# Two of five chunk pairs of a SwiGLU layer as seven block products, with the second matrix product's steps among them and TensorE's order pinned

## The chip, the cores and the metric

The kernel runs on one core of a Trainium2 chip. The metric is the device time of one execution in microseconds. Its engines are named as in the profile: PE (TensorE: matmuls and transposes), PEld (its weight loads, which overlap matmuls), DVE (VectorE), ACT (ScalarE), POOL (GpSimd) and SP (SyncE, whose queue starts nearly all DMAs here). L12 is line 12 of the kernel.

## The reference

Two layers of a decoder trunk, each a feed-forward network (FFN), a token mixer and another FFN, with a normalization after each. 256 tokens, width 1024, FFN width 2816; all in float32.

```python
def swiglu(x, wg, wu, wd):
    return (jax.nn.silu(x @ wg) * (x @ wu)) @ wd
...
for l in range(DEPTH):
    x = layer_norm(ALPHA * x + 0.5 * swiglu(x, ffn_wg[l, 0], ffn_wu[l, 0], ffn_wd[l, 0]), ln_g[l, 0], ln_b[l, 0])
    m = token_mix(x, w_in[l], w_out[l], ...)
    x = layer_norm(ALPHA * x + m, ln_g[l, 1], ln_b[l, 1])
    x = layer_norm(ALPHA * x + 0.5 * swiglu(x, ffn_wg[l, 1], ffn_wu[l, 1], ffn_wd[l, 1]), ln_g[l, 2], ln_b[l, 2])
```

The change concerns the four FFNs alone.

## The kernel before

**Tiles.** The 256 tokens are two token tiles t = 0, 1 of 128. The FFN width is cut into 11 chunks of 256. For a chunk, "gate and up" is one product: x (128 tokens, 1024 wide) times a 1024x512 block that holds 256 columns of wg and 256 of wu. It takes eight contraction steps of 128 and gives one PSUM bank of 128x512. Its first half goes through silu, the product of both halves is the chunk's hidden value hh (128x256). hh is transposed, and "down" multiplies it by 256 rows of wd into two banks (acc) that gather the result of all eleven chunks.

**Precision.** Each float32 matmul is three matmuls in a shorter format (fp32r): a number is split into a high part and a low part, and high x high, high x low and low x high are added (`mm3`, L183-186). So each weight tile must be split. `split_half` (L157-168) does it: SP's queue loads a raw tile of 128x1024 (512 KB, L163) into one of three buffers `raw`, ACT writes the high part `wh` (L166), DVE subtracts it for the low part `wl` (L167). There are eight buffers of `wh` and eight of `wl`. The raw buffer is free again when DVE has read it, the split buffers when PE has used them for both token tiles. x is transposed by PE and split in the same way (`make_xT`, L217, with the split at L189 and L190); so is hh (L212, then L189/L190).

**Units.** A list of units, of two weight tiles each, fixes the order of the weights: for chunk c its two gate-and-up units (q = 0, 1: the two halves of the contraction), then the down unit of chunk c-1. `unit(t)` (L177) hands out the next one to token tile t and makes one more ahead (`AHEAD = 1`).

**Order.** `ffn_steps` (L263-325) is a generator for one token tile: gate and up of a chunk (`glu`), the down of the chunk before, the transposes of hh (`h_T`). `ffn` (L762-803) runs the two generators alternately, up to three steps apart. The two token tiles use the same weight unit soon after each other. The program is written in this order, but a scheduler then places each engine's instructions by its own estimate of times, so that transposes stand in the midst of other products. Banks of PSUM: two acc for each token tile, and one g and one tr for each, where tr takes transposes.

**Ends.** After the last down `layer_norm` (L238-260) adds and normalizes x in two halves on DVE, with small steps elsewhere, and `make_xT` transposes it for the next layer. In the second FFN of layer 0 the next user is the first FFN of layer 1 (around 490 us in the trace). In the first FFN some constants of the mixer (`late_constants`) are loaded from SP's queue in its middle.

The three lines that all matmuls of the products come from:

```python
PE.matmul(ps, xh, wh, start=start, stop=False)
PE.matmul(ps, xh, wl, start=False, stop=False)
last_pe[0] = PE.matmul(ps, xl, wh, start=False, stop=stop)
```

## Time and profile before

| | |
|---|---|
| median of 3 runs | 1008.43 us (1007.34 to 1010.68) |
| profiled execution | 1007.14 us |
| its span | 1005.4 us |
| TensorE's granted clock | 0.998 |
| DMA moved | 178.80 MB, 178 GB/s on average |

The page gives the busy time of each engine, and in 40 slices of the span how busy each was and what the DMAs moved. The four FFNs lie at about 20 to 186, 322 to 489, 500 to 688 and 816 to 996 us; the mixers lie between the first and second and between the third and fourth, and the second FFN is followed directly by the third. A group row reads: line, engine, operation, out <- in, shape, count, then busy time and the mean of one in ns, then how long the engine was idle just before and what ended that. A row of the timeline reads: start and duration in us, engine, line, operation, and in brackets the wait before it and what ended it. A matmul of 512 columns is shown with 0.39 us, but these overlap: the pace is the distance of their starts.

### The profile page before, as it was taken

To read this page: it belongs to the slowest core of one execution; us is meant where nothing else is said; L and a number is where in the kernel's file an instruction comes from. 1 tells how busy PE (TensorE), PEld (TensorE's weight loads), DVE (VectorE), ACT (ScalarE), POOL (GpSimd) and SP (SyncE) were. 2 spreads that over 40 slices of the span, in tenths; PEclk is the share of its full clock that TensorE was granted. 3 is DMA by queue.
4 is the path that set the end of the run, shared out by engine and by line. 5 is a ranking of instruction groups with operands and counts; after the bars stand their busy time and mean duration, and the time that the engine had idled before them with its cause. 6 is when DMAs were issued, how large, how long until landed. Compare 5 with 4: busy or idle time off the path is not lost.

```text
span 1005.4 us, 12883 instructions
## 1 busy us (share of the span) xinstructions
PE 991.1 (99%) x4755; PEld 804.1 (80%) x4755; DVE 630.8 (63%) x1051; ACT 491.1 (49%) x788; POOL 35.4 (4%) x50
## 2 busy tenths in 40 slices
PE   8999999999999999999999999999999999999996
PEld 5888888878778888888878888887778788888885
DVE  5545645688869555555775545459888685545455
ACT  5535544366744444444444444435666454444440
POOL 0000000020001000000000000001100010000000
PEclk9999999999999999999999999999999999999999
DMA  7787665365515655556475565645524176565541
GB/s 234 236 254 255 214 195 170 120 196 173 161 55 172 228 186 190 187 188 189 146 243 197 174 197 178 196 151 189 180 84 147 45 230 207 181 195 179 194 152 42
DMA packets 51871, 178.80 MB, mean 178 GB/s; under 512 B 6624, under 2 KB 7648, under 8 KB 51552
## 3 DMA queue, kind: packets, MB, share of 16 engines
q1 hardware_dynamic: 49968, 171.23, 53.2%
q0 software_dynamic: 1840, 6.75, 2.3%
q8 instruction: 37, 0.61, 0.2%
q14 instruction: 26, 0.21, 0.1%
HBM read 176.91 MB, written 1.05 MB: 177 GB/s over the span
## 4 chain that ended last, share of the span: by engine, by line
PE 89%; DVE 5%; DMA 3%; issue 1%; ACT 1%; SPq 0%; DVEq 0%; ACTq 0%
PE g L184 15%; PE g L186 15%; PE g L185 15%; PE acc L184 11%; PE acc L186 11%; PE acc L185 11%; PE tr L212 4%; DMA raw<-in_wgu 2%; PE acc L203 2%; DVE wl L167 2%; PE tr L203 1%; ACT wh L166 1%; PE tr L458 1%; PE acc L200 1%; DMA x<-in_x 1%
## 5 line engine op out<-in xcount | busy, mean ns | idle before, releaser
L167 DVE TENSOR_TENSOR wl<-raw,wh 128x1024 fp32r<-128x1024 f32 (+2 forms) x321 | 388.4, 1212 | 255.6 <-ACT wh L166 244.2
L166 ACT ACTIVATE wh<-raw 128x1024 fp32r<-128x1024 f32 (+2 forms) x321 | 336.1, 1049 | 286.6 <-PE acc L186 103.3
L184 PE MATMUL g<-wh,xh 128*128 128x512 f32 (+1 forms) x736 | 292.6, 398 | 0.0
L186 PE MATMUL g<-wh,xl 128*128 128x512 f32 (+1 forms) x736 | 286.1, 389 | 0.0
L185 PE MATMUL g<-wl,xh 128*128 128x512 f32 (+1 forms) x736 | 285.4, 388 | 0.4 <-DVE wl L167 0.4
L186 PEld LDWEIGHTS g<-wh,xl 128*128 128x128 f32 x736 | 138.4, 188 | 28.2
L185 PEld LDWEIGHTS g<-wl,xh 128*128 128x128 f32 x736 | 138.7, 189 | 26.9 <-DVE wl L167 1.5
L184 PEld LDWEIGHTS g<-wh,xh 128*128 128x128 f32 x736 | 138.4, 188 | 25.9 <-ACT wh L166 0.7
L184 PE MATMUL acc<-wh,hi 128*128 128x512 f32 x352 | 138.5, 393 | 0.0
L186 PE MATMUL acc<-wh,lo 128*128 128x512 f32 x352 | 137.7, 392 | 0.0
L185 PE MATMUL acc<-wl,hi 128*128 128x512 f32 x352 | 137.3, 390 | 0.0
L186 PEld LDWEIGHTS acc<-wh,lo 128*128 128x128 f32 x352 | 66.1, 188 | 13.6
L184 PEld LDWEIGHTS acc<-wh,hi 128*128 128x128 f32 x352 | 66.1, 188 | 13.5 <-ACT hi L189 0.4
L185 PEld LDWEIGHTS acc<-wl,hi 128*128 128x128 f32 x352 | 66.2, 188 | 13.4
L282 ACT ACTIVATE sg<-g 128x256 f32<-128x256 f32 x80 | 30.5, 382 | 75.2 <-PE g L186 74.9
L189 ACT ACTIVATE hi<-tr 128x256 fp32r<-128x256 f32 x88 | 32.9, 374 | 66.4 <-PE tr L212 66.4
L190 DVE TENSOR_TENSOR lo<-tr,hi 128x256 fp32r<-128x256 f32 x88 | 37.0, 421 | 39.2 <-ACT hi L189 39.2
L185 PE MATMUL acc<-wl,xh 128*128 128x512 f32 x128 | 51.2, 400 | 0.5 <-DVE wl L167 0.5
L184 PE MATMUL acc<-wh,xh 128*128 128x512 f32 x128 | 51.2, 401 | 0.0
L186 PE MATMUL acc<-wh,xl 128*128 128x512 f32 x128 | 51.0, 398 | 0.0
L284 DVE SCALAR_TENSOR_TENSOR hh<-sg,g 128x256 f32<-128x256 f32 x80 | 33.4, 417 | 26.5 <-ACT sg L282 26.5
L252 POOL TENSOR_TENSOR ve<-ve,mhalf 128x1 f32<-128x1 f32 x12 | 11.5, 957 | 755.9 <-DVE ve L251 755.9
(207 smaller groups left out, 826.8 us busy)
## 6 DMA issues: line engine op xcount, KB each, us to landing
raw<-in_wgu SPq DMA_DIRECT2D x175, 512.0 KB, 3.9
raw<-in_wd SPq DMA_DIRECT2D x88, 512.0 KB, 3.9
raw<-in_win SPq DMA_DIRECT2D x32, 512.0 KB, 4.0
raw<-in_wout SPq DMA_DIRECT2D x16, 512.0 KB, 3.6
lnp_ln_g<-in_ln_g POOLq DMA_DIRECT2D x5, 512.0 KB, 5.1
lnp_ln_b<-in_ln_b POOLq DMA_DIRECT2D x5, 512.0 KB, 5.7
raw<-in_win SPq DMA_DIRECT2D x8, 296.0 KB, 2.9
x<-in_x SPq DMA_DIRECT2D x4, 256.0 KB, 4.9
```

The source lines that it names most:

```text
L166: ACT.activation(out=wh[:, s], in_=raw[:, s], func=AF.Copy)
L167: DVE.tensor_sub(out=wl[:, s], in0=raw[:, s], in1=wh[:, s].bitcast(F32))
L184: PE.matmul(ps, xh, wh, start=start, stop=False)
L185: PE.matmul(ps, xh, wl, start=False, stop=False)
L186: last_pe[0] = PE.matmul(ps, xl, wh, start=False, stop=stop)
L189: ACT.activation(out=hi, in_=src, func=AF.Copy)
L190: DVE.tensor_sub(out=lo, in0=src, in1=hi.bitcast(F32))
L203: PE.matmul(out, lhsT, rhs, start=False, stop=True, skip_group_check=True)
L212: last_pe[0] = PE.transpose(p[:, i * 128:(i + 1) * 128], s, ident)
L252: POOL.tensor_tensor(out=ve[:, 1:2], in0=ve[:, 0:1], in1=mhalf[:, 0:1], op=ALU.pow)
L282: ACT.activation(out=sg, in_=ps[:, 0:256], func=AF.Silu)
L284: DVE.scalar_tensor_tensor(out=hh, in0=sg, scalar=0.5, in1=ps[:, 256:512], op0=ALU.mult, op1=ALU.mult)
```

## The change

**Grouping.** The eleven chunks are now groups: pairs (0,1), (2,3), (6,7) and the single chunk 10 are computed as before ("n"); the pairs (4,5) and (8,9) are done in seven block products ("s").

**Block products.** For a pair of chunks, x is a 2x2 matrix of blocks: token tile t by half q of the contraction, 128x512 each. The weights are a 2x2 matrix too: half q by chunk, 512x512 each. That is eight block products of 4 steps x 3 matmuls = 12 matmuls. The Strassen-Winograd scheme needs seven: three of plain blocks of x with a plain or combined block of weights, and four of sums of blocks of x. Sums of x are made once per FFN (`make_sums`, and copies of the transposed x at L307 and L310 in `make_xT`). Differences of weights are made for each pair, in float32, ahead of the split (`less`, L143). To that end four raw tiles are kept for longer, in buffers that the mixer had to itself: two `fa` and, from the tag pT, two `fc`. The sums of results are made from banks by DVE with high priority (L452, 453, 459, 464, 469), with two copies on ACT.

**Downs.** In the groups "n" no down is done. The four downs due stand between the block products of the next "s" group, in the order of `SEVEN`: product, down, product, down, two products, down, two products, down, product. Downs of chunks 8, 9 and 10 come at the end, for token tile 0 and then for tile 1 (`end`). hh of a pair is transposed by four transposes into one bank (`h_T`), where it was two and two.

**Order pinned, banks.** From the pair (2,3) to chunk 10 (`middle`) each matmul of these products is pinned (`tc.keep_in_program_order`): the scheduler leaves PE's order as written. Units are then made three ahead, otherwise one. The four banks g0, g1, tr0, tr1 are now a free list in an FFN. The constants of the mixer are loaded after the group (6,7) of the first FFN.

The diff, cut to its core:

```diff
+GROUPS = (("n", 0, 1), ("n", 2, 3), ("s", 4, 5), ("n", 6, 7), ("s", 8, 9), ("n", 10))
+SEVEN = (None, 0, None, 1, None, None, 2, None, None, 3, None)
-    "P": (("P",), 3),
+    "P": (("P",), 4),
+    def seven(l, f, c):
...
+        def less(a, b, to):
+            for x, y, z in zip(a, b, to):
+                DVE.tensor_sub(out=z, in0=x, in1=y)
...
+        def f1():
+            for h, a in enumerate(gate_up(l, f, c, 0)):
+                load(A, [a], mix, name="fa", tag=f"qs{h}", bufs=1)
+            return parts(A)
+        def f2():
+            load(B, gate_up(l, f, c + 1, 0), wp, name="raw", bufs=3)
+            less(B, A, A)
+            return parts(A)
+        def f3():
+            load(C, gate_up(l, f, c + 1, 1), mix, name="fc", tag="pT", bufs=3)
+            less(C, B, B)
+            return parts(B)
+        def f4():
+            less(C, A, A)
+            return parts(A)
+        def f5():
+            load(E, gate_up(l, f, c, 1), wp, name="raw", bufs=3)
+            return parts(E)
+        def f6():
+            return parts(C)
+        def f7():
+            less(E, A, A)
+            return parts(A)
...
+    def make_sums(sums):
+        out = []
+        s1, a11, a12, a21 = sums["s"], sums[0, 0], sums[0, 1], sums[1, 0]
...
+        parts(s1, 0)
+        DVE.tensor_sub(out=s1, in0=s1, in1=a11)
+        DVE.tensor_sub(out=a21, in0=a11, in1=a21)
+        parts(a21, 1)
+        parts(s1, 2)
+        DVE.tensor_sub(out=a12, in0=a12, in1=s1)
+        parts(a12, 3)
...
+            self.free = [("g", 0), ("g", 1), ("tr", 0), ("tr", 1)]
...
+            (w1, b1), (w5, b5) = self.bank(), self.bank()
+            self.product(b1, a[0][0])
+            with tc.high_priority():
+                c11 = f32("c11")
+                ACT.activation(out=c11, in_=b1, func=AF.Copy)
+            for t in range(2):
+                self.h_T(t, c // 2 - 1)
+            down()
+            self.product(b5, s1)
+            down()
+            w7, b7 = self.bank()
+            self.product(b7, s3)
+            self.product(b1, s2, False)
+            with tc.high_priority():
+                u = f32("u")
+                ACT.activation(out=u, in_=b1, func=AF.Copy)
+                c22 = f32("c22")
+                DVE.tensor_add(out=c22, in0=b5, in1=u)
+                DVE.tensor_add(out=c22, in0=b7, in1=c22)
+            self.gated(1, c + 1, c22)
+            down()
+            w2, b2 = self.bank()
+            self.product(b2, a[0][1])
+            with tc.high_priority():
+                DVE.tensor_add(out=c11, in0=b2, in1=c11)
+            self.gated(0, c, c11)
+            self.product(b5, s4, False)
...
+            down()
+            self.product(b7, a[1][1], False)
...
+        def end(self, t, sums):
+            self.down(t, NCH - 3)
+            self.h_T(t, NCH // 2)
+            self.down(t, NCH - 2)
+            self.down(t, NCH - 1)
+            layer_norm(t, self.accs[t], self.l, self.i)
+            if (self.l, self.i) != (L - 1, 2):
+                make_xT(t, sums=sums)
```

**PE in the middle of an FFN.** Before, a down of one chunk (acc from wh, wl and hi, lo) is followed by the two transposes of one chunk's hh and another down:

```order
L184 MATMUL acc_337<-wh,hi 128x512
L185 MATMUL acc_337<-wl,hi 128x512
L186 MATMUL acc_337<-wh,lo 128x512
L184 MATMUL acc_338<-wh,hi 128x512
L185 MATMUL acc_338<-wl,hi 128x512
L186 MATMUL acc_338<-wh,lo 128x512
L212 MATMUL tr_629<-ident,hh 128x128 x2
L184 MATMUL acc_370<-wh,hi 128x512
L185 MATMUL acc_370<-wl,hi 128x512
```

Now, at the start of the first block stage, the first block product (L418, into bank tr_545) ends, the transposes of two chunks stand together for each token tile, and the first down follows:

```order
L418 MATMUL tr_545<-wh,xh_100 128x512
L418 MATMUL tr_545<-wl,xh_100 128x512
L418 MATMUL tr_545<-wh,xl_101 128x512
L487 MATMUL g_573<-ident,hh_443 128x128 x4
L487 MATMUL g_582<-ident,hh_459 128x128 x4
L264 MATMUL acc_591<-wh,hi 128x512
L265 MATMUL acc_591<-wl,hi 128x512
L266 MATMUL acc_591<-wh,lo 128x512
```

What moved: a block product, which needs no hh, now stands ahead of the transposes, and these come in fours. L264-266 are the lines that were L184-186.

**PE at the end of the second FFN.** Before, token tile 0's new x (x_102) is transposed among the last downs of tile 1, which come after a whole chunk's product into g_4377:

```order
L184 MATMUL acc_3183<-wh,hi 128x512
L185 MATMUL acc_3183<-wl,hi 128x512
L186 MATMUL acc_3183<-wh,lo 128x512
L184 MATMUL acc_3184<-wh,hi 128x512
L212 MATMUL tr_4363<-ident,x_102 128x128 x4
L212 MATMUL acc_4370<-ident,x_102 128x128 x4
L212 MATMUL tr_4406<-ident,hh 128x128 x2
L185 MATMUL acc_3184<-wl,hi 128x512
```

Now tile 1 has only its three downs (8, 9, 10) left, and the transposes (x_98 is tile 0's x) stand in the second of them:

```order
L487 MATMUL tr_4434<-ident,hh_4325 128x128 x2
L264 MATMUL acc_3423<-wh,hi 128x512
L265 MATMUL acc_3423<-wl,hi 128x512
L266 MATMUL acc_3423<-wh,lo 128x512
L264 MATMUL acc_3424<-wh,hi 128x512
L265 MATMUL acc_3424<-wl,hi 128x512
L292 MATMUL tr_4404<-ident,x_98 128x128 x4
L292 MATMUL acc_4413<-ident,x_98 128x128 x4
L266 MATMUL acc_3424<-wh,lo 128x512
```

The whole chunk's product of 24 matmuls no longer stands in between.

**DVE at the first block stage.** Before, low parts of weights (L167) alternate with low parts of the transposed hh (L190) and gates (L284):

```order
L190 TENSOR_TENSOR lo<-tr_363,hi 128x256
L167 TENSOR_TENSOR wl<-raw,wh 128x1024
L190 TENSOR_TENSOR lo<-tr_384,hi 128x256
L167 TENSOR_TENSOR wl<-raw,wh 128x1024 x4
L284 SCALAR_TENSOR_TENSOR hh<-sg,g_391 128x256
```

Now the differences (L143) stand there too, and low parts come from the kept tiles (L220) as well as from fresh ones (L232):

```order
L143 TENSOR_TENSOR raw<-fc,raw 128x1024
L143 TENSOR_TENSOR fa<-fc,fa 128x1024
L270 TENSOR_TENSOR lo<-g_573,hi 128x512
L270 TENSOR_TENSOR lo<-g_582,hi 128x512
L143 TENSOR_TENSOR fa<-fc,fa 128x1024
L232 TENSOR_TENSOR wl<-raw,wh 128x1024
L220 TENSOR_TENSOR wl<-raw,wh 128x1024 x2
L220 TENSOR_TENSOR wl<-fa,wh 128x1024 x2
L232 TENSOR_TENSOR wl<-raw,wh 128x1024 x2
```

Each kept tile is written over by its difference, so `fa` and `raw` appear as outputs of L143.

**SP's queue at the start.** Before, raw tiles are loaded in the order of their use:

```order
L163 DMA raw<-in_wgu 128x1024 x7
L163 DMA raw<-in_wd 128x1024 x2
L163 DMA raw<-in_wgu 128x1024 x4
L163 DMA raw<-in_wd 128x1024 x2
L163 DMA raw<-in_wgu 128x1024 x4
```

Now the tiles that the first block stage keeps stand among the first groups' loads:

```order
L228 DMA raw<-in_wgu 128x1024 x3
L139 DMA fa<-in_wgu 128x1024 x2
L228 DMA raw<-in_wgu 128x1024 x3
L139 DMA fc<-in_wgu 128x1024 x2
L228 DMA raw<-in_wgu 128x1024 x3
L139 DMA fc<-in_wgu 128x1024
L228 DMA raw<-in_wgu 128x1024 x6
L228 DMA raw<-in_wd 128x1024 x2
```

The third `fc` is the second block stage's first tile, in the third buffer of its tag. Over the whole program PE has 96 matmuls of 512 columns fewer, 3687 where there were 3783.

More of the change, by code (lines that the diff above doesn't have):

```diff
@@ L172, in split_weights @@
         while len(made) < min(n, len(units)):
-            made.append([split_half(src, w) for src, w in units[len(made)]])
+            made.append(units[len(made)]())
     pos = [0, 0]
+    ahead = [1]
     def unit(t):
@@ L179, in unit, with both, pe @@
         pos[t] += 1
-        split_weights(u + 1 + AHEAD)
+        split_weights(u + 1 + ahead[0])
         return made[u]
+    def both():
+        u = unit(0)
+        assert unit(1) is u
+        return u
+    pinned = [False]
+    def pe(ins):
+        if pinned[0]:
+            tc.keep_in_program_order(ins)
+        last_pe[0] = ins
     def mm3(ps, xh, xl, wh, wl, start, stop):
-        PE.matmul(ps, xh, wh, start=start, stop=False)
-        PE.matmul(ps, xh, wl, start=False, stop=False)
-        last_pe[0] = PE.matmul(ps, xl, wh, start=False, stop=stop)
+        pe(PE.matmul(ps, xh, wh, start=start, stop=False))
+        pe(PE.matmul(ps, xh, wl, start=False, stop=False))
+        pe(PE.matmul(ps, xl, wh, start=False, stop=stop))
     def split(hi, lo, src):
@@ L223, in make_xT, with parts @@
             split(xh[:, 4 * q:4 * q + 4, :], xl[:, 4 * q:4 * q + 4, :], p.rearrange("p (a b) -> p a b", a=4))
+            if sums is not None:
+                if (t, q) != (1, 1):
+                    f = sums[t, q] = mix.tile([128, 512], F32, name=f"a{t}{q}", tag=("c40", "c41", "at011")[2 * t + q], bufs=1)
+                    ACT.activation(out=f, in_=p, func=AF.Copy)
+                else:
+                    f = sums["s"] = mix.tile([128, 512], F32, name="s1", tag="vblk", bufs=1)
+                    DVE.tensor_add(out=f, in0=p, in1=sums[1, 0])
+    def make_sums(sums):
+        out = []
+        s1, a11, a12, a21 = sums["s"], sums[0, 0], sums[0, 1], sums[1, 0]
+        big = cst.tile([128, 2, 2, 4, 128], F32R, name="sb", tag="s_w1")
+        def parts(f, i):
+            tl = cst.tile([128, 2, 4, 128], F32R, name=f"sa{i}", tag=("ksh", "ksl")[i]) if i < 2 else big[:, i - 2]
+            split(tl[:, 0], tl[:, 1], f.rearrange("p (a b) -> p a b", a=4))
+            out.append((tl[:, 0], tl[:, 1]))
+        parts(s1, 0)
[5 more added lines that the diff above has]
+        parts(a12, 3)
+        s1, s3, s2, s4 = out
+        return s1, s2, s3, s4
     lnp = {}
@@ L761, in run, with ffn @@
             k += 1
-    def ffn(l, i):
-        gens = [ffn_steps(t, l, i) for t in range(2)]
-        n = 3 * NCH
-        done = [0, 0]
-        def go(t, k):
-            run(gens[t], k)
-            done[t] += k
+    def ffn(l, i, sums, after):
+        f = Ffn(l, i, sums)
         if (l, i) == (0, 0):
@@ L773, in ffn @@
             load_x(0, 0)
-            make_xT(0, (0,))
+            make_xT(0, (0,), sums)
             with tc.issue_after(last_pe[0].ins):
                 warm_up()
-            first = split_half(*units[0][0], 2, (lambda: load_x(0, 1), lambda: load_x(1, 0)))
+            first = split_half(gate_up(0, 0, 0, 0)[0], 1024, 2, (lambda: load_x(0, 1), lambda: load_x(1, 0)))
             with tc.issue_after(last_pe[0].ins):
-                make_xT(0, (1,))
+                make_xT(0, (1,), sums)
             load_x(1, 1)
-            made.append([first, split_half(*units[0][1])])
-            gens[0] = ffn_steps(0, l, i)
-            go(0, 1)
+            made.append([first, split_half(gate_up(0, 0, 0, 0)[1], 1024)])
+            f.glu(0, 0, 0)
             with tc.issue_after(x1_after[0].ins):
-                make_xT(1)
-            gens[1] = ffn_steps(1, l, i)
-            go(1, 1)
-            go(0, 1)
-            go(1, 1)
-            go(0, 1)
-        else:
-            go(0, LEAD)
-        while done[0] < n - LEAD + 1:
-            go(1, min(2, done[0] - done[1] - 1) if done[0] - done[1] > 2 else 1)
-            if done[0] - done[1] <= 1:
-                go(0, 1)
-            if not m0 and done[0] >= 12:
-                with tc.issue_after(last_dma[0].ins):
-                    late_constants()
-                    m0.append(Mix(0))
-                    ln_params(0, 0)
-        go(0, n - done[0])
-        return gens[1], n - done[1]
+                make_xT(1, sums=sums)
+            f.glu(1, 0, 0)
+            f.glu(0, 0, 1)
+            f.glu(1, 0, 1)
+            f.glu(0, 1, 0)
+        else:
+            f.glu(0, 0, 0)
+            f.glu(0, 0, 1)
+            f.glu(0, 1, 0)
+            f.glu(1, 0, 0)
+            f.glu(1, 0, 1)
+        f.glu(0, 1, 1)
+        f.glu(1, 1, 0)
+        f.glu(1, 1, 1)
+        f.middle()
+        for t in range(2):
+            f.end(t, after)
     m0 = []
-    rest = None
+    sums = {}
     for l in range(L):
-        rest = ffn(l, 0)
-        run(*rest)
+        ffn(l, 0, sums, None)
         m = m0[0] if l == 0 else Mix(l)
@@ L828, in build @@
             assert next(g, "end") == "end"
-        rest = ffn(l, 2)
-        run(*rest)
+        nxt = {}
+        ffn(l, 2, m.sums, nxt)
+        sums = nxt
 def _layout(inp):
```

225 lines of the change are left out of this document (156 added, 69 removed).

## The prediction

> **What bounds the kernel now.** I read the page's busy times first, then TensorE's list of waits, then a dense stretch of the timeline.
>
> ```profile
> PE 991.1 (99%) x4755; PEld 804.1 (80%) x4755; DVE 630.8 (63%) x1051; ACT 491.1 (49%) x788; POOL 35.4 (4%) x50
> L186 PEld LDWEIGHTS g<-wh,xl 128*128 128x128 f32 x736 | 138.4, 188 | 28.2
> L212 PE MATMUL tr<-ident,hh 128*128 128x128 f32 x176 | 33.8, 274 | 1.3 <-DVE hh L284 1.3
> ```
>
> ```profile
> PE tr L212 <- DVE hh L284: 1.3, 3, 0.6
> PE acc L102 <- DVE zw L105: 1.2, 1, 1.2
> PE acc L212 <- DMA x<-in_x: 1.1, 1, 1.1
> ...
> PE tr L212 <- DVE x L257: 0.2, 1, 0.2
> ```
>
> A busy share of 99% may hide gaps, since overlapping matmuls are counted to modelled ends. So the waits matter more: the longest total on one cause is 1.3 us in 1005.4. The pace settles it: starts of matmuls with 512 columns in the middle of the third feed-forward layer (FFN):
>
> ```profile
> 600.73 0.39 PE L185 MATMUL acc<-wl,hi 128*128 128x512 f32 x1
> ...
> 602.09 0.39 PE L185 MATMUL acc<-wl,hi 128*128 128x512 f32 x1
> ```
>
> Six matmuls in 1.36 us are 0.2267 us each, back to back. The other engines of the same FFN wait for TensorE: this is ACT, about to split the next weight tile.
>
> ```profile
> 602.07 1.06 ACT L166 ACTIVATE wh<-raw 128x1024 fp32r<-128x1024 f32 x1 [2.74 <-PE acc L186]
> 603.43 1.06 ACT L166 ACTIVATE wh<-raw 128x1024 fp32r<-128x1024 f32 x1 [0.30 <-PE acc L186]
> ```
>
> The weight was there, but no buffer of its split form was free until TensorE had used one. So TensorE bounds, and the splitting runs as far ahead as eight buffers allow.
>
> **What goes.** A pair of chunks is eight products of a 128x512 block of x with a 512x512 block of weights, 12 matmuls each. Seven products leave out 12. Two pairs in each of four FFNs: 2 x 4 x 12 = 96 matmuls, and the instruction order has indeed 96 fewer with 512 columns. At 0.2267 us that is **-21.8 us**. If weight loads set the pace (188 ns above) it would be 96 x 0.188 = 18.0; the pace is measured, so I take 21.8. The 176 transposes of hh stay, merged into fours. The three waits for hh (1.3 us) go: in plain groups hh now has 24 matmuls (5.4 us) of cover, in block stages 12 (2.7 us). **-1.3 us.** In the block stages the chain can be longer than the cover: after a running ACT pass (1.06) silu 0.38, after a running DVE pass (1.23) the gate 0.42, together 3.1 us. That is 0 to 0.4 us eight times, up to 3.2; the order puts the gate ahead of the next splits, so I take 0.
>
> These rows price that chain and all that comes:
>
> ```profile
> L167 DVE TENSOR_TENSOR wl<-raw,wh 128x1024 fp32r<-128x1024 f32 x311 | 380.9, 1227 | 248.1 <-ACT wh L166 236.8
> L284 DVE SCALAR_TENSOR_TENSOR hh<-sg,g 128x256 f32<-128x256 f32 x80 | 33.4, 417 | 26.5 <-ACT sg L282 26.5
> L246 DVE SCALAR_TENSOR_TENSOR x<-x,acc 128x512 f32<-128x512 f32 x24 | 16.3, 684 | 11.8 <-PE acc L186 11.6
> L190 DVE TENSOR_TENSOR xl<-tr,xh 128x512 fp32r<-128x512 f32 x12 | 8.2, 685 | 0.9 <-ACT xh L189 0.9
> L166 ACT ACTIVATE wh<-raw 128x1024 fp32r<-128x1024 f32 x311 | 329.3, 1060 | 268.1 <-PE acc L186 103.3 <-PE g L186 85.6 <-DMA raw<-in_wgu 43.8
> L282 ACT ACTIVATE sg<-g 128x256 f32<-128x256 f32 x80 | 30.5, 382 | 75.2 <-PE g L186 74.9 <-DVE wl L167 0.3
> L189 ACT ACTIVATE xh<-tr 128x512 fp32r<-128x512 f32 x12 | 7.1, 593 | 12.1 <-PE tr L212 12.1
> ```
>
> **What the block stages add.** DVE makes 8 differences and 14 + 8 low parts of 128x1024 (no row shows a difference of two weight tiles; the low part has the same shape and operands): 30 x 1.227 = 36.8 us. Five adds from banks (0.684), four gates (0.417) and two low parts of h (0.685) make 6.5 more: 43.3 us. TensorE has 84 + 96 matmuls, 40.8 us, and eight transposes of at most 33.8/176 = 0.19 us: 42.3 us. ACT has 22 x 1.06 plus about 4. So DVE is 1.0 us longer than TensorE there; in the plain group before it, TensorE has 96 matmuls (23.3 us with transposes) and DVE 12.9. Both together: TensorE 65.6, DVE 56.2. The eight split buffers carry a lead over: a tile may be made once TensorE has finished with the eighth tile before it. A late place: the second tile of the fourth down gets its buffer when the fourth product ends, 23.1 us into the stage (four products 10.9, two downs 10.9, transposes). ACT 1.06 and DVE 1.23, behind three result passes (1.8), make it ready at 27.2; it is read 12 + 24 matmuls and half a token tile's down later, near 35. **0 us**, with 7 to spare.
>
> The raw tiles are the other supply:
>
> ```profile
> DMA to landing us min/median/max: 2.8/3.8/4.5
> ```
>
> One tile holds a raw buffer for 3.8 + 1.06 + 1.23 and some 0.2 of semaphores, 6.3 us. Stage and group need 20 tiles through three buffers, but while the second or the fourth block of a pair is kept for later differences only one buffer is left, for four tiles. 16 x 6.3/3 + 4 x 6.3 = 58.8 us, under 65.6. **0 us** again.
>
> **The first FFN's constants** now load in front of the second block stage. Before, they did this:
>
> ```profile
> 69.25 0.85 SPq L163 DMA_DIRECT2D raw<-in_wd  x2
> ```
>
> ```profile
> 76.77 1.06 ACT L166 ACTIVATE wh<-raw 128x1024 fp32r<-128x1024 f32 x1 [3.30 <-DMA raw<-in_wd]
> ```
>
> The first row is from SP's timeline, the second from ACT's: 7.5 us from issue to use instead of 3.8, hidden by the lead. Behind them stands now a down through one raw buffer; its second tile comes 6.3 us after its first. By the same reckoning it is ready about when it is needed: 0 to 3 us, I take **+0.5**.
>
> **The start.** Four tiles for the first block stage (two at first, two more soon after) go out in SP's queue ahead of weights that are needed sooner.
>
> ```profile
> 14.62 1.23 DVE L167 TENSOR_TENSOR wl<-raw,wh 128x1024 fp32r<-128x1024 f32 x1 [0.40 <-ACT wh L166]
> 17.53 1.22 DVE L167 TENSOR_TENSOR wl<-raw,wh 128x1024 fp32r<-128x1024 f32 x1 [1.69 <-ACT wh L166]
> 20.17 1.23 DVE L167 TENSOR_TENSOR wl<-raw,wh 128x1024 fp32r<-128x1024 f32 x1 [1.42 <-ACT wh L166]
> ```
>
> ```profile
> 21.98 0.48 PE L184 MATMUL g<-wh,xh 128*128 128x512 f32 x1
> ```
>
> ```profile
> GB/s 234 236 254 255 214 195 170 120 196 173 161 55 172 228 186 190 187 188 189 146 243 197 174 197 178 196 151 189 180 84 147 45 230 207 181 195 179 194 152 42
> ```
>
> The tile made at 17.53 is used at 21.98 (3.2 us to spare), the next six matmuls later, at 23.3 (1.9 to spare). Two tiles of 512 KB at the 255 GB/s of the fourth slice are 4.1 us: 0.9 to 2.2 us late. In DVE's queue the sums of x are eight passes of 0.685, 5.5 us, ahead of the same tiles, and the idle stretches in these rows hold 3.5 of it: 2.0 late. The delays overlap. **+2.0 us**, from 0 (if the loads fit into idle DMA time) to 5 (added up). In the other three FFNs the sums are made when tiles lie ready, and the early loads fall into the attention's end or the FFN before: 0 to 2 us each, I take 0.5. **+1.5 us.**
>
> **Ends of FFNs.** Token tile 0's normalization is now covered by the other's three downs alone:
>
> ```profile
> 490.67 0.39 PE L186 MATMUL acc<-wh,lo 128*128 128x512 f32 x1
> ...
> 503.17 0.39 PE L184 MATMUL acc<-wh,xh 128*128 128x512 f32 x1
> ```
>
> ```profile
> 492.86 1.41 DVE L255 SCALAR_TENSOR_TENSOR x<-x,mv,lnp_ln_g 128x512 f32<-128x512 f32 x2
> 494.18 2.35 DVE L167 TENSOR_TENSOR wl<-raw,wh 128x1024 fp32r<-128x1024 f32 x2
> 496.45 1.40 DVE L257 SCALAR_TENSOR_TENSOR x<-x,ve,lnp_ln_b 128x512 f32<-128x512 f32 x2
> ...
> 499.24 0.68 DVE L190 TENSOR_TENSOR xl<-tr,xh 128x512 fp32r<-128x512 f32 x1
> ```
>
> Before, 12.5 us of TensorE work lay between the last down and the first use of the new x, which was ready after 9.3. Now it is 36 matmuls and ten transposes, 10.1 us. But the transposes of x stand after 17 of these matmuls and two transposes, 4.2 us, and x's first half came after 6.5, or 4.1 without the two weight passes in the middle. The new order has none in the middle; the second half comes 0.7 later. 0 to 2.3 us at three ends; 0.4 each, **+1.2 us**.
>
> **Sum.** -21.8 - 1.3 + 0.5 + 2.0 + 1.5 + 1.2 = -17.9 us. The profiled execution took 1007.14 us (span 1005.4 and 1.7 around it): 989.2. The median of the runs shown is 1008.43, 1.3 above it, so the same sum for a median gives 990.5; I say **990**.
>
> **A price below the pace.** Were a removed matmul worth no more than its weight load, 188 ns, the gain is 18.0 us in place of 21.8: 994. Against it stands the pace itself. The Trainium skill, "TensorE: Matmul & The Clock Gate", section "Back-to-back issue gap", says that a stream of loads and matmuls of 512 columns is spaced 131 ns. By that figure the removal would be worth 12.6 us and the time about 999; the rows above, at 226.7 ns, do not agree.
>
> **Rivals.** *Block stages bound by DVE*: the lead isn't carried over and each lasts as DVE's 43.3 us, 1.0 longer: 8 us in all, 998. For it: DVE's row would come near 83% (630.8 + 8 x (14 x 1.227 + 3.4) + 4 x 5.5 = 817 us). Against it: the waits of ACT on TensorE above. *Pinned order*: TensorE can no longer pull other matmuls forward, and waits about 1.5 us in each of eight stages, for hh or a bank: +12, 1002. Against it: banks are read long before they are reused. *Raw buffers run dry*, the slower side: a buffer's 6.3 us grows with both queues busy. The balance tips at 65.6/(16/3 + 4) = 7.0 us; at 7.7 stage and group last 71.9, 6.3 more, eight times 50 us: 1040. For it: the 7.5 us landing above, and the early loads. Against: 4.5 was the longest landing in a whole FFN, which makes 7.0 just then. *The change doesn't remove what it says* is excluded by the count of matmuls.
>
> **Chances.** Forecast 0.72; DVE-bound stages 0.10; pinned waits 0.08; dry raw buffers 0.07; the lower price 0.03. A measurement of this kernel can tell about 0.3% (3 us) from no change. Forecast, lower price and DVE-bound stages are faster, pinned waits mostly (0.03 of them less than 3 us): faster 0.88, same 0.04, and slower 0.08 with the dry buffers. The low end is the sum with every unknown cost at nothing, 984; the high end takes in 998 and most of the pinned case, 1001. What is left out is the dry buffers, part of the pinned case and little else.
>
> **What would show it.** Right: TensorE's pace stays 0.227 us through the stages, its waits total some microseconds, DVE stands near 83%, and ACT's splits still wait for TensorE. Wrong: matmuls of a product waiting for wl or wh (DVE-bound), ACT waiting for DMA in the stages (raw buffers), transposes of hh or result adds next to gaps of TensorE (pinned). A first FFN much longer than the third would put the loss on the early loads.

## The result, and the profile after

The changed kernel takes 993.5 us (median of four runs, 989.4 to 995.5) beside 1008.9 us before: a ratio of 0.984, interval 0.981 to 0.988. That is faster by 1.6%, 15.9 us on a base of 1008, where 17.9 was forecast. The profiled execution took 994.04 us with a span of 991.9. Of all the executions below one is left out of the ratios: the kernel with the differences on GpSimd once took 1624.4 us, with a granted clock of 0.556. The page's busy line and TensorE's list of waits, the same two views as before:

```profile
PE 971.4 (98%) x4659; PEld 789.1 (80%) x4659; DVE 784.3 (79%) x1195; ACT 549.0 (55%) x840; POOL 34.8 (4%) x50
```

```profile
PE g L487 <- DVE hh L404: 4.6, 4, 1.9
PE acc L265 <- DVE wl L232: 2.0, 3, 1.0
PE g L265 <- DVE wl L232: 1.7, 3, 0.7
```

TensorE has the 96 matmuls fewer, VectorE stands at 79% where some 83% was foreseen, and the longest total on one cause is now 4.6 us: transposes of hh that wait for the gate on VectorE (L404), four times, up to 1.9 us. They were 1.3 us before, and the forecast had them at zero.

A table by stage (from the first matmul, or the last one of the layer before, to the last down or output matmul of the layer, us) shows where the time came from:

| | FFN 1 | mixer | FFN 2 | FFN 3 | mixer | FFN 4 |
|---|---|---|---|---|---|---|
| before | 190.9 | 117.6 | 187.5 | 189.2 | 119.0 | 186.0 |
| after | 187.2 | 119.7 | 183.3 | 186.0 | 118.3 | 182.3 |

The FFNs give 14.8 us, the mixers take 1.4 back. 24 matmuls are worth 5.4 us; no FFN gave more than 4.2.

One of the four waits, in the third FFN. TensorE's timeline first:

```profile
545.26 0.40 PE L418 MATMUL tr<-wh,xl 128*128 128x512 f32 x1
545.49 0.60 PE L487 MATMUL g<-ident,hh 128*128 128x128 f32 x4
547.95 0.66 PE L487 MATMUL g<-ident,hh 128*128 128x128 f32 x4 [1.86 <-DVE hh L404]
...
550.86 0.63 PE L264 MATMUL acc<-wh,hi 128*128 128x512 f32 x1
551.29 0.63 PE L265 MATMUL acc<-wl,hi 128*128 128x512 f32 x1
```

Token tile 0's four transposes run, tile 1's wait 1.86 us. And then the matmuls start 0.43 us apart instead of 0.23. The table of stretches says why (the first numbers are the stretch, its length, and busy times of PE, PEld, DVE, ACT and POOL with counts; then come the granted clock, the DMA share and GB/s):

```profile
546.00:549.00 3.00, 1.14 (x7) 0.96 (x7) 3.00 (x5) 1.13 (x3) 0.00 (x0) 0.93 0.08 19
549.00:552.00 3.00, 3.00 (x8) 2.33 (x8) 1.36 (x4) 1.46 (x3) 0.00 (x0) 0.50 0.39 156
552.00:555.00 3.00, 3.00 (x14) 2.49 (x14) 3.00 (x3) 2.41 (x3) 0.00 (x0) 1.00 0.26 63
```

After the wait the clock was granted at 0.50 for 3.4 us (548.60 to 552.02 us). Half of that stretch, 1.7 us, is lost, so this wait cost TensorE 3.6 us in all.

The silu (ScalarE, L403) that the late gate needed, and what VectorE did meanwhile:

```profile
543.84 0.37 ACT L403 ACTIVATE sg<-g 128x256 f32<-128x256 f32 x1
```

```profile
543.75 1.22 DVE L220 TENSOR_TENSOR wl<-fa,wh 128x1024 fp32r<-128x1024 f32 x1
544.88 0.41 DVE L404 SCALAR_TENSOR_TENSOR hh<-sg,g 128x256 f32<-128x256 f32 x1
545.21 1.22 DVE L143 TENSOR_TENSOR fa<-fc,fa 128x1024 f32<-128x1024 f32 x1
546.35 1.22 DVE L232 TENSOR_TENSOR wl<-raw,wh 128x1024 fp32r<-128x1024 f32 x1
547.48 0.41 DVE L404 SCALAR_TENSOR_TENSOR hh<-sg,g 128x256 f32<-128x256 f32 x1
```

The second silu was done at 544.2. Its gate could have followed the first at 545.3. But the order in VectorE's queue had a difference (L143) and a low part of 1.22 us each ahead of it, which TensorE didn't wait for then: it began 2.3 us later.

### The profile page after: what moved, and what is told of

The parts are those of the page before. It is cut to its first block, busy times and chain, and to the rows that moved or that the text cites. A ratio compares the mean times of both kernels' runs of the same rounds, so it can differ in the third digit from the quotient of the medians.

```text
span 991.9 us, 12822 instructions
## 1 busy us (share of the span) xinstructions
PE 971.4 (98%) x4659; PEld 789.1 (80%) x4659; DVE 784.3 (79%) x1195; ACT 549.0 (55%) x840; POOL 34.8 (4%) x50
## 4 chain that ended last, share of the span: by engine, by line
PE 30%; DVE 10%; DMA 7%; ACT 2%; issue 2%; DVEq 0%; ACTq 0%; SPq 0%
PE acc L266 5%; PE acc L264 5%; PE acc L265 5%; DMA raw<-in_wgu 5%; DVE wl L232 3%; PE tr L418 3%; PE g L418 2%; DMA raw<-in_wd 2%; PE g L265 1%; DVE fa L143 1%; DVE wl L220 1%; PE g L266 1%; PE g L264 1%; ACT wh L231 1%; PE tr L292 1%
## 5 line engine op out<-in xcount | busy, mean ns | idle before, releaser
L232 DVE TENSOR_TENSOR wl<-raw,wh 128x1024 fp32r<-128x1024 f32 (+2 forms) x257 | 308.3, 1206 | 113.0 <-ACT wh L231 112.3
L231 ACT ACTIVATE wh<-raw 128x1024 fp32r<-128x1024 f32 (+2 forms) x257 | 267.9, 1045 | 223.0 <-DMA raw<-in_wgu 76.0
L264 PE MATMUL acc<-wh,hi 128*128 128x512 f32 x352 | 139.4, 396 | 0.0
L265 PE MATMUL g<-wl,xh 128*128 128x512 f32 (+1 forms) x320 | 122.9, 384 | 1.7 <-DVE wl L232 1.7
L264 PE MATMUL g<-wh,xh 128*128 128x512 f32 (+1 forms) x320 | 123.7, 387 | 0.0
L266 PE MATMUL g<-wh,xl 128*128 128x512 f32 (+1 forms) x320 | 122.5, 383 | 0.0
L219 ACT ACTIVATE wh<-fa 128x1024 fp32r<-128x1024 f32 x64 | 65.2, 1051 | 45.8 <-DVE fa L143 16.9
L220 DVE TENSOR_TENSOR wl<-fa,wh 128x1024 fp32r<-128x1024 f32 x64 | 76.4, 1219 | 4.6 <-ACT wh L219 4.3
L264 PEld LDWEIGHTS acc<-wh,hi 128*128 128x128 f32 x352 | 66.5, 189 | 13.9 <-ACT wh L231 0.4
L265 PEld LDWEIGHTS g<-wl,xh 128*128 128x128 f32 x320 | 60.3, 188 | 13.7 <-DVE wl L232 3.1
L264 PEld LDWEIGHTS g<-wh,xh 128*128 128x128 f32 x320 | 60.1, 188 | 11.7 <-issue 0.8
L266 PEld LDWEIGHTS g<-wh,xl 128*128 128x128 f32 x320 | 60.1, 188 | 10.8
L264 PE MATMUL tr<-wh,xh 128*128 128x512 f32 x160 | 63.3, 396 | 0.0
L143 DVE TENSOR_TENSOR fa<-raw,fa 128x1024 f32<-128x1024 f32 x32 | 38.6, 1221 | 18.8 <-DMA raw<-in_wgu 18.8
L264 PE MATMUL acc<-wh,xh 128*128 128x512 f32 x128 | 50.7, 398 | 0.4 <-ACT wh L231 0.4
```

The lines of the kernel that those rows point to most:

```text
L143: DVE.tensor_sub(out=z, in0=x, in1=y)
L219: ACT.activation(out=wh[:, :w], in_=raw[:, :w], func=AF.Copy)
L220: DVE.tensor_sub(out=wl[:, :w], in0=raw[:, :w], in1=wh[:, :w].bitcast(F32))
L231: ACT.activation(out=wh[:, s], in_=raw[:, s], func=AF.Copy)
L232: DVE.tensor_sub(out=wl[:, s], in0=raw[:, s], in1=wh[:, s].bitcast(F32))
L264: pe(PE.matmul(ps, xh, wh, start=start, stop=False))
```

## The experiments

The theory after this reading: the removed matmuls are worth TensorE's pace, and part of it is lost because differences of weights stand ahead of ready gates in VectorE's queue. The rivals: VectorE's load as such, the pinned order, or a price of a matmul below the pace. All kernels ran beside runs of the kernel before; where times are turned into differences, each is its ratio times 1008.

| kernel | median us | ratio to before, interval |
|---|---|---|
| changed | 993.5 | 0.9842 (0.9806 to 0.9877) |
| eight plain products, new frame | 1003.6 | 0.9957 (0.9943 to 0.9972) |
| the same, transposes in twos | 1008.1 | 0.9997 (0.9988 to 1.0006) |
| one pair of seven products | 995.1 | 0.9878 (0.9865 to 0.9891) |
| differences left out | 985.9 | 0.9783 (0.9769 to 0.9797) |
| transposes later, block stage | 992.6 | 0.9833 (0.9811 to 0.9855) |
| transposes later, both | 994.4 | 0.9864 (0.9846 to 0.9883) |
| differences on GpSimd | 1026.4 | 1.0176 (1.0149 to 1.0202) |
| order not pinned | 992.2 | 0.9846 (0.9831 to 0.9860) |
| plain blocks for sums | 992.8 | 0.9858 (0.9836 to 0.9880) |
| differences behind the gates | 986.7 | 0.9786 (0.9774 to 0.9799) |
| all splits behind silu and gate | 992.0 | 0.9857 (0.9833 to 0.9882) |
| differences behind the gates, sums in two tiles | 986.8 | 0.9782 (0.9755 to 0.9809) |

**Eight plain products in the new frame.** The block stages without Strassen's scheme; the weights come in the order of these products, and no sums of x are made (both left out here):

```diff
-GROUPS = (("n", 0, 1), ("n", 2, 3), ("s", 4, 5), ("n", 6, 7), ("s", 8, 9), ("n", 10))
+GROUPS = (("n", 0, 1), ("n", 2, 3), ("e", 4, 5), ("n", 6, 7), ("e", 8, 9), ("n", 10))
...
+                if kind == "e":
+                    for n in range(4):
+                        self.glu(0, cs[n // 2], n % 2)
+                        if n == 0:
+                            for t in range(2):
+                                self.h_T(t, cs[0] // 2 - 1)
+                        self.glu(1, cs[n // 2], n % 2)
+                        for t in range(2):
+                            self.down(t, cs[0] - 4 + n)
+                    continue
```

> The two pairs (4,5) and (8,9) are computed as eight plain products, in the frame of the changed kernel: same groups, downs between the products, order pinned, free list of banks, ends. Sums of x, differences of weights and sums of results are left out, with their buffers' use; the transposes of hh still stand 12 matmuls behind the last plain group's. Theory (a removed matmul is worth TensorE's pace of 0.2267 us, the frame is worth nothing): 993.5 + 21.8 less the waits that the changed kernel shows for hh and wl (4.6 and some 2): 1008 to 1011, like the kernel before. Rival (the new arrangement, not the seven products, brings the time): below 1003. Rival (a removed matmul is worth less, 131 ns): about 1000 to 1006.

1003.6 us. It fell between: the frame alone, which was to be worth nothing, gives 4.3 us. So the seven products give 11.6 us, not 21.8. Two questions follow: where the frame's gain comes from, and what eats nearly half of the seven products' worth.

**Transposes in twos.** In that kernel the eight transposes of a pair of chunks and both token tiles are taken apart into four runs of two among the products:

```diff
-                        if c % 2 == 0 and q == 0:
-                            for t in range(2):
-                                self.h_T(t, c // 2 - 1)
+                            if c % 2 == 0:
+                                self.h_T(t, c // 2 - 1, q)
```

(`h_T` got a third argument, which of the two chunks; the block stages likewise.)

> The kernel with eight plain products in the new frame (1003.6 us), but hh is transposed two by two again, in 88 runs that stand among the products, as the kernel before has them. Theory (a run of two costs TensorE 0.253 us with the slower starts after it, a run of eight 0.906; so merging is worth some 2.3 us of the frame's 4.2): 1005 to 1007. Rival (merging is worth nothing, and the frame's gain comes from elsewhere): 1003 to 1004.5. Rival (merging is all of the gain): 1007.5 or more.

1008.1 us, ratio 0.9997: the time of the kernel before. Taking the merging of transposes back takes the frame's whole gain back. A run of two in the kernel before, and a run of eight in the changed one:

```profile
24.61 0.39 PE L186 MATMUL g<-wh,xl 128*128 128x512 f32 x1
24.84 0.38 PE L212 MATMUL tr<-ident,hh 128*128 128x128 f32 x2
24.97 0.48 PE L184 MATMUL g<-wh,xh 128*128 128x512 f32 x1
25.29 0.39 PE L185 MATMUL g<-wl,xh 128*128 128x512 f32 x1
...
26.44 0.39 PE L184 MATMUL g<-wh,xh 128*128 128x512 f32 x1
```

```profile
58.62 0.39 PE L418 MATMUL tr<-wh,xl 128*128 128x512 f32 x1
58.85 1.03 PE L487 MATMUL g<-ident,hh 128*128 128x128 f32 x8
59.64 0.48 PE L264 MATMUL acc<-wh,hi 128*128 128x512 f32 x1
59.95 0.39 PE L265 MATMUL acc<-wl,hi 128*128 128x512 f32 x1
...
61.11 0.39 PE L264 MATMUL acc<-wh,hi 128*128 128x512 f32 x1
```

In each piece seven long matmuls start. They would take 1.59 us at the pace; with two transposes it is 1.83, with eight 2.49: 0.24 and 0.90 us. By these two pieces, 88 runs of two cost 21.1 us, 20 runs of eight and 8 of two 19.9. That is 1 to 2 of the 4 us; a wait of 1.3 us for a gate, which the kernel with twos has and the one with eights has not, is a further part. The intervals leave 2.3 to 5.8 us for the difference of the two kernels, so the rest of the 4 us stays open.

**One pair.** The first pair in seven products, the second in eight (the same edit for one group alone):

> The changed kernel with the second of the two pairs, (8,9), as eight plain products in the same frame: 48 matmuls of the 96 come back, half of the differences go. Theory (each pair is worth the same): half way between the kernel with two pairs (about 992.5) and that with none (1003.6): 997 to 999. Rival (the second block stage of the first FFN, behind the constants, and the FFN's late stages bring less): 995 or less; rival (the first stage brings less): 1000 or more.

995.1 us: the first pair gives 8.0 us (0.9957 to 0.9878), the second then 3.6. That is nearer to the rival on the second stage than to equal pairs, but the intervals leave the second anything from nothing to 7.4 us. Nor can the pairs be told apart so simply: with the second stage changed, the scheduler's order in the first changed too, and this kernel shows one wait for a gate, of 0.6 us, where the changed kernel has four. Its third FFN adds something: a difference and a low part stand ahead of the second gate there as well, but that gate ends at 546.2, 1.7 us earlier than in the changed kernel, and TensorE doesn't wait. So this order costs time only where VectorE is late when it reaches the gate.

**Differences left out.**

```diff
             for x, y, z in zip(a, b, to):
-                DVE.tensor_sub(out=z, in0=x, in1=y)
+                pass
```

> The changed kernel without the differences of the weights (64 passes of VectorE of 1.22 us, 78 us in all): the products take the blocks as loaded, everything else stays. Theory: VectorE's work is covered but for the waits that the profile shows for hh (4.6 us) and part of those for wl (3.7): 986.5 to 989.5. Rival (stages bound by VectorE): over 8 us less, 985.5 or lower. Rival (the differences cost nothing, TensorE waits for other reasons): 992 or more.

985.9 us: 5.9 us less than the changed kernel by the ratios (intervals: 2.1 to 9.8). The products take the blocks as loaded, so this kernel doesn't compute the layer. TensorE waits for no gate in this kernel, and its clock is never down in an FFN; 4.6 us of waits and 1.7 of slow clock are 6.3. That fits the theory, but 78 us of VectorE's work are gone too: whether load or place had cost the time needed the next ones.

**Transposes later.** In a block stage the transposes of hh stand behind the first down:

```diff
-            for t in range(2):
-                self.h_T(t, c // 2 - 1)
             down()
+            for t in range(2):
+                self.h_T(t, c // 2 - 1)
```

> One edit to the changed kernel: the transposes of the last plain pair's hh stand behind the block stage's first down instead of in front of it (24 more matmuls of cover). Theory (the 4.6 us that TensorE waits for hh are a fault of place: two differences stand ahead of the gate in VectorE's queue, and nothing else is late): 989, between 988 and 990.5. Rival (VectorE bounds the stage, and what is not waited for at the transposes is waited for at the next wl): 992 to 994.5.

992.6 us, the rival's time, and no gain that these runs can tell. The wait went elsewhere:

```profile
PE tr L487 <- DVE u L476: 2.6, 1, 2.6
PE g L487 <- DVE u L476: 2.2, 2, 1.2
```

Now the gate that the block stage makes last (L476) is late. ScalarE's and VectorE's timelines at one of these places:

```profile
587.54 1.06 ACT L231 ACTIVATE wh<-raw 128x1024 fp32r<-128x1024 f32 x1 [2.27 <-PE g L266]
588.51 0.40 ACT L475 ACTIVATE u<-u 128x256 f32<-128x256 f32 x1
```

```profile
586.45 0.68 DVE L469 TENSOR_TENSOR u<-g,u 128x512 f32<-128x512 f32 x1
588.64 1.23 DVE L232 TENSOR_TENSOR wl<-raw,wh 128x1024 fp32r<-128x1024 f32 x1 [1.50 <-ACT wh L231]
589.78 0.42 DVE L476 SCALAR_TENSOR_TENSOR u<-u 128x256 f32<-128x256 f32 x1
```

The sum u was ready at 587.1. Its silu stood in ScalarE's queue behind a weight split that itself waited 2.27 us for a buffer, then its gate behind that tile's low part. VectorE was idle for 1.5 us of it, so at this place the gate isn't late by VectorE's load, which was the rival's reason.

**Both later.** The transposes in a plain group are moved too:

```diff
-                        if c % 2 == 0 and q == 0:
-                            for t in range(2):
-                                self.h_T(t, c // 2 - 1)
+                            if c % 2 == 0 and q == 1:
+                                self.h_T(t, c // 2 - 1)
```

> The changed kernel with both transposes of hh later: in a block stage behind the first down, and in a plain group behind the second half of its first chunk instead of the first half. Theory (with the first edit alone, the wait only passed to the gate that the block stage makes last, 4.8 us at three places; now both are covered by 24 matmuls or more): 988 to 990. Rival (VectorE is behind, and any cover only moves the wait to the next weight tile): 992 to 994.

994.4 us: no gain again. More cover alone doesn't help. The late gate now holds a bank that the next product needs (PE tr L264, 2.1 us). VectorE's timeline there:

```profile
413.53 1.22 DVE L143 TENSOR_TENSOR fa<-raw,fa 128x1024 f32<-128x1024 f32 x1 [2.14 <-DMA raw<-in_wgu]
414.67 0.41 DVE L404 SCALAR_TENSOR_TENSOR hh<-sg,tr 128x256 f32<-128x256 f32 x1
```

The difference ahead of the gate waits for its DMA, and VectorE stands still with it.

**Differences on GpSimd.**

```diff
-                DVE.tensor_sub(out=z, in0=x, in1=y)
+                POOL.tensor_sub(out=z, in0=x, in1=y)
```

> The changed kernel with all 64 differences of weights on GpSimd instead of VectorE. Theory (the differences cost 6 us by delaying gates and low parts in VectorE's queue): if a pass on GpSimd takes under 3 us, VectorE falls to about 720 us busy and the time to 986 to 990. Rival (the chain difference, high part, low part is what is late): a slower pass makes it longer, TensorE waits for wh and wl of the products, 996 or more.

1026.4 us, slower than before. A difference takes 3.0 us there, and TensorE waits for the gates more than ever:

```profile
L143 POOL TENSOR_TENSOR fa<-raw,fa 128x1024 f32<-128x1024 f32 x32 | 97.0, 3041 | 353.7 <-DMA raw<-in_wgu 298.6 <-issue 27.3 <-DVE hh L404 25.6
```

```profile
PE g L487 <- DVE hh L404: 22.6, 9, 8.6
```

VectorE's timeline at the longest:

```profile
57.15 2.44 DVE L220 TENSOR_TENSOR wl<-fa,wh 128x1024 fp32r<-128x1024 f32 x1 [3.38 <-ACT wh L219]
59.51 0.41 DVE L404 SCALAR_TENSOR_TENSOR hh<-sg,g 128x256 f32<-128x256 f32 x1
65.44 2.39 DVE L220 TENSOR_TENSOR wl<-fa,wh 128x1024 fp32r<-128x1024 f32 x1 [5.52 <-ACT wh L219]
...
68.89 0.41 DVE L404 SCALAR_TENSOR_TENSOR hh<-sg,g 128x256 f32<-128x256 f32 x1
```

Here the second gate stands behind a low part that waits 5.5 us for ScalarE and, through it, for GpSimd's difference. The gate's silu stood in ScalarE's queue behind the split of that same tile, which waited 7.0 us for the difference. So one late difference held up a gate that doesn't need it, in two queues. This is the late chain of the rival, but TensorE met it at the gates, not at wh and wl. Load and place aren't told apart by this run: VectorE has 64 passes fewer, but it is busy for 788.5 us, as with them (784.3), since its passes beside GpSimd's take up to twice as long.

**Differences behind the gates.** Nothing left out; the differences of the third and fourth block may not pass the last plain gate in VectorE's queue:

```diff
-            less(C, B, B)
+            with tc.issue_after(last_gate[-1].ins):
+                less(C, B, B)
...
-            less(C, A, A)
+            with tc.issue_after(last_gate[-1].ins):
+                less(C, A, A)
...
```

(`last_gate` gathers the gates of the plain groups.)

> One edit to the changed kernel: the differences of a block stage's third and fourth weight blocks are queued on VectorE behind the gate of the plain group before it. Nothing is left out and nothing else moves by hand. Theory (the 6 us that the differences cost are not VectorE's load but their place in its queue ahead of a ready gate; the wait of 1.9 us also halves TensorE's clock for some 4 us): the waits for hh go, the clock stays up, and the time is that of the kernel without differences, 986 to 988.5. Rival (VectorE's load is the cost, so a wait turns up at the next late gate or low part, as in the two kernels with later transposes): 991 to 995.

986.7 us, the time of the kernel without any differences (985.9), and faster than the changed kernel by 5.6 us (intervals: 1.8 to 9.4). TensorE's waits now begin with

```profile
PE acc L268 <- DVE wl L235: 1.6, 2, 1.0
PE g L268 <- DVE wl L235: 1.4, 2, 0.7
```

and the third FFN's VectorE does what was wanted:

```profile
542.16 0.41 DVE L407 SCALAR_TENSOR_TENSOR hh<-sg,g 128x256 f32<-128x256 f32 x1
542.50 2.35 DVE L143 TENSOR_TENSOR raw<-fc,raw 128x1024 f32<-128x1024 f32 x2
```

VectorE is as busy as in the changed kernel (786.8 us, 80%). So with the load as it is, the place of these differences cost the 5.6 us: that is shown by the experiment. The FFNs last 187.1, 181.6, 182.7 and 180.4 us in its trace; with eight plain products they last 188.9, 186.3, 186.7 and 185.1.

**All splits behind silu and gate.** The same for every weight split and difference in the pinned part, on both engines:

```diff
...
+            if pinned[0] and last_gate:
+                with tc.issue_after(last_gate[-1].ins), tc.issue_after(last_silu[-1].ins):
+                    made.append(units[len(made)]())
...
```

> The changed kernel with every weight split and difference that the program makes after a silu and gate, in the pinned middle of an FFN, queued behind that silu on ScalarE and that gate on VectorE. Theory (place, not load): like the kernel with only the differences behind the gates, 986 to 988.5, and steadier. Rival (the queues need to run ahead of the gates, and strict order makes low parts late): 993 or more.

992.0 us: strict order gives the gain back. Behind the constants of the first FFN the second down now waits for its second tile:

```profile
135.39 0.49 PE L270 MATMUL acc<-wh,hi 128*128 128x512 f32 x1 [1.25 <-ACT wh L233]
136.65 0.54 PE L271 MATMUL acc<-wl,hi 128*128 128x512 f32 x1 [0.77 <-DVE wl L234]
136.99 0.63 PE L272 MATMUL acc<-wh,lo 128*128 128x512 f32 x1
```

and again the starts after it are 0.42 us apart.

**Order not pinned.**

```diff
-            pinned[0] = True
+            pinned[0] = False
```

> The changed kernel with TensorE's order left to the scheduler in the middle of the FFNs too. Theory: the pinned order costs no more than the waits seen, so the scheduler can win 4 us at most and may lose some: 989 to 997. Rival (pinning costs 1.5 us in each of eight stages): 980 to 984.

992.2 us, the same ratio as the changed kernel, though its trace has only 0.7 us of waits for hh. Pinning costs and gives nothing that these runs can tell.

**Plain blocks for the sums.**

```diff
-            self.product(b5, s1)
+            self.product(b5, a[1][0])
...
-            self.product(b7, s3)
-            self.product(b1, s2, False)
+            self.product(b7, a[1][0])
+            self.product(b1, a[1][1], False)
...
-            self.product(b5, s4, False)
+            self.product(b5, a[1][1], False)
```

> The changed kernel, but the four products with sums of x take plain blocks of x in their place (the sums are still made and not used). Only the tile changes that TensorE loads as the stationary operand. In the changed kernel's trace matmuls with these sums start 0.232 us apart, those with x 0.2267. Theory (the spacing hangs on the operand's tile): all at 0.2267, 384 x 0.0055 = 2.1 us less: 990 to 992. Rival (the spacing belongs to the place in the stage, beside VectorE's work): still 0.232, 993 to 994.

In the changed kernel a product of a sum of x, and one of x, start at

```profile
65.20 0.39 PE L418 MATMUL tr<-wh,sa 128*128 128x512 f32 x1
...
66.36 0.63 PE L418 MATMUL tr<-wh,sa 128*128 128x512 f32 x2
```

```profile
56.12 0.39 PE L418 MATMUL tr<-wh,xh 128*128 128x512 f32 x1
...
57.48 0.39 PE L418 MATMUL tr<-wh,xh 128*128 128x512 f32 x1
```

Five steps in 1.16 us are 0.232 us each (0.233 in the mean over all of them), six in 1.36 are 0.2267. With plain blocks all products of the block stages start 0.2267 apart: the spacing does hang on the operand, 384 x 0.006 = 2.3 us. The time, 992.8 us, does not show it: this kernel had other waits (2.4 us for a split behind the constants), and the expected 2.1 us is within its spread.

**Sums in two tiles.** On top of the kernel with the differences behind the gates (`small` is two new tiles, one for high parts and one for low parts):

```diff
-            tl = cst.tile([128, 2, 4, 128], F32R, name=f"sa{i}", tag=("ksh", "ksl")[i]) if i < 2 else big[:, i - 2]
-            split(tl[:, 0], tl[:, 1], f.rearrange("p (a b) -> p a b", a=4))
...
+            if i < 2:
+                h, w = small[0][:, i], small[1][:, i]
+            else:
+                h, w = big[:, i - 2, 0], big[:, i - 2, 1]
+            split(h, w, f.rearrange("p (a b) -> p a b", a=4))
```

> The kernel with the differences behind the gates, and one more edit: the high and low parts of the sums s1 and s2 (the second operand kept being s3 and s4) lie in two tiles instead of one tile for both parts; s3 and s4 stay as they are, as a control. Matmuls with sums as the operand start 0.2328 us apart, those with x, whose high and low parts lie in two tiles, 0.2267. Theory (high and low part in one tile make the slower spacing): s1 and s2 at 0.2267, the others at 0.233, 1 us less: 985 to 986.5. Rival (something else about these operands, their place in memory for one): all stay at 0.233, 986 to 987.5.

(The sums are made in the order s1, s3, s2, s4; those moved are s1 and s3.) 986.8 us, and the spacing stays: 0.2325 and 0.2335 for the high and low parts moved, 0.2331 for the control. It is not the common tile. What it is stays open; another place in memory wasn't tried.

## Why the prediction came out

The time, 993.5, lies in the range 984 to 1001 and near 990. What bounds the kernel and what the change removes were read rightly. That the number came so near is partly luck: a gain of 4 us that the working put at nothing and a loss of 5.6 us that it put at nothing nearly cancelled.

- **"What goes": -21.8 us at the pace of 0.2267.** The price is right, less 2.3 us for the slower sums. From eight products (0.9957) to seven with the differences behind the gates (0.9786) it is 17.2 us (intervals: 15.3 to 19.2). 17.2 + 2.3 leaves 2.3 to the whole, and some half of that is the start of the first FFN (below). The lower price doesn't fit: between these two kernels the second and the fourth FFN gain 4.7 us each, where 24 matmuls less the slower sums are 4.9 at the pace and 3.9 at 0.188 us.
- **"The 176 transposes of hh stay, merged into fours"**, at no cost or gain. That step failed: with the merging taken back the frame's 4 us are gone.
- **"The three waits for hh (1.3 us) go", and "0 to 0.4 us eight times, I take 0".** This failed. The chain was counted with one running pass ahead of the gate, "the order puts the gate ahead of the next splits". In the third FFN's trace a difference and a low part stood ahead of the second gate. The four waits are 4.6 us, and the slow clock after one of them 1.7, which the working hadn't at all. With the differences behind the gates the time is 5.6 us less.
- **Stages bound by VectorE** was given 0.10, and the forecast 0 us for its load. Right: at 80% busy with the differences in a better place, the waits of 0.5 us or more that TensorE has left on VectorE lie at the first FFN's start (15.52 us) and in the mixers (218.84, 226.44 and 703.28 us), none in a block stage.
- **The raw tiles**, 0 us: right but for the down behind the constants (next point), the one place in a block stage where TensorE waits 0.5 us or more for a weight. But the margin shrank. "ACT's splits still wait for TensorE" was to be a sign of being right, and "ACT waiting for DMA in the stages" one of dry raw buffers. The second is what shows, without that rival's 50 us: the splits, which mostly waited for TensorE before, now wait mostly for loads:

```profile
ACT wh L231 <- DMA raw<-in_wgu: 76.0, 60, 3.5
ACT wh L231 <- DMA raw<-in_wd: 70.5, 50, 4.5
ACT wh L231 <- PE acc L266: 35.3, 19, 6.5
```

- **The constants, +0.5 (0 to 3)**: the second tile of that down was late by 0.18 and then 1.03 us, where it was foreseen. That is 1.2 us. With the differences behind the gates no wait of 0.5 us is left there. In the changed kernel:

```profile
133.92 0.39 PE L266 MATMUL acc<-wh,lo 128*128 128x512 f32 x1
134.33 0.49 PE L264 MATMUL acc<-wh,hi 128*128 128x512 f32 x1
135.58 0.50 PE L265 MATMUL acc<-wl,hi 128*128 128x512 f32 x1 [0.76 <-DVE wl L232]
```

- **The start, +2.0.** About half of it. From the start of the FFN (as in the table by stage) to its first down, the seven-product kernel should take 2.72 us less than eight products do, since 12 matmuls fewer stand there. With the differences behind the gates and the sums in two tiles, this stretch is 2.66 to 2.70 us shorter in the last three FFNs and 1.55 in the first. So the start cost 1.1 to 1.2 us, and the **+1.5** of the other starts almost nothing. Most of the 1.1 is one early weight tile: TensorE waits 0.44 us for its high part and 1.02 for its low part, where with eight products it waits 0.53 for the low part alone. The trace of the kernel with the differences behind the gates can't be used for this: its clock was granted at 0.50 from 8.82 to 12.23 us, and its first FFN lasts 187.1 us, where it lasts 185.6 with the sums in two tiles and a full clock from 4.42 us on.
- **The ends, +1.2**, were too high as well: in that kernel the last three FFNs come within 0.2 to 0.9 us of the 4.9 that their 24 matmuls are worth after the slower sums.
- **Pinned order** fell. Its sign, gaps of TensorE at transposes of hh, did show; but without pinning the ratio is the same.
- **The chances** of the five cases give 0.90 for faster, 0.03 for the same and 0.07 for slower by the prediction's own split, not 0.88, 0.04 and 0.08.

Sum on 1008: -4.3 for the frame, -17.2 for the seven products, +5.6 for the gates' place, -15.9 in all. These are steps from kernel to kernel, so they add up by construction.

## What to carry to other kernels

An engine that works at 80% can hold up one at 98% through the order in its queue: look which short instruction of a critical chain stands behind a long one that nobody needs yet, and order these two. Ordering everything gave the gain back here. Where a wait only moves when its cover grows, move the late instruction itself. And when a change also rearranges, run the rearrangement alone: here it was worth a quarter of the gain and hid that the main part gave little more than half of its worth.

## What the runs showed of the hardware

- **The clock after a wait.** After waits of 1.86 us (above), 2.1 and 2.6 us (the two kernels with later transposes) and 1.25 and 0.77 us close together (the strict order), the clock was granted at 0.50 for 3.4 us each time, and four to eight matmuls of 512 columns started 0.427 us apart. The length of the wait doesn't decide it. After 1.67 us, in the fourth FFN of the changed kernel, the clock stayed full; so it did after 2.03 and 0.77 us close together in the kernel with plain blocks (at 137.19 and 138.45 us). With the differences on GpSimd four waits of 2.63 or 2.64 us stand in front of transposes of hh: after those that end at 379.68, 570.47 and 878.88 us the clock was at 0.50, after the one that ends at 449.42 us it was full. The clock records of the traces show what differs: in each trace the clock changes only at whole multiples of 3.413 us from its first rise (in the changed kernel 159 and 160 of them after it). So it seems to matter how a wait lies to these steps; how idle a step must be isn't shown. The Trainium skill, "TensorE: Matmul & The Clock Gate", section "What's actually happening", has the array fall to half speed after an idle window of about 3.4 us. The trace agrees on the half speed and on the length, but shows it after waits shorter than that. In its section on transposes the page says that these don't count as busy for the gate. By that the 2.9 us from the first transpose at 545.49 to the next matmul at 548.36 would count, which is nearer; but the strict order's place has no transposes, and no run here takes the two apart.
- **Transposes in the stream.** A run of two cost 0.24 us, one of eight 0.90: 0.12 and 0.11 each. In the two pieces above the first matmul after a run starts 0.32 us before the next, and the five or six after it start about 0.231 apart on average, before the pace is 0.2267 again.
- **VectorE beside GpSimd.** While GpSimd made differences, a low part on VectorE took 2.44 us instead of 1.22 (the row at 57.15). The Trainium skill, "GPSIMD Engine Reference", section "1. Specifications", says that the two share their way to memory where a VectorE instruction has two inputs there; this agrees.
- **The operand's place.** Matmuls with the sums of x as the loaded operand start 0.233 us apart, all others 0.2267, with equal weight loads of 188 ns. The cause isn't known.
